# A recurrence phase with another order of its steps, and its triangular solve in blocks of 16 rows that PE joins in pairs

## The chip, the cores and the metric

The kernel runs on one core of a Trainium2 chip. The metric is the device time of one execution in microseconds, as the median of several. Engines are named as in the profile: PE (matmul), DVE (VectorE), ACT (ScalarE), POOL (GpSimd) and SP (SyncE, which here issues most DMAs).

## The reference: what is computed

One decoder layer for 2048 tokens of width 1024. A projection feeds two groups of heads: a state-space mixer (SSD) and an RWKV-7 mixer with 8 heads of 64. Their outputs are projected, normalised and added to the input, and a gated convolutional feed-forward layer with another residual follows. The change lies in the RWKV-7 recurrence, which per head and token is:

```
sa = S @ a_t
S  = S * w_t + outer(sa, b_t) + outer(v_t, k_t)
y  = S @ r_t
```

The kernel computes it by chunks of 64 tokens. Within a chunk the vectors `sa` depend on one another through a strictly lower triangular 64x64 matrix for each head, so a unit triangular system has to be solved for each head and chunk. That is the triangular solve below.

## The kernel before

**Phases.** `phase_R` runs first (RWKV-7 for all tokens), then `phase_S` (the SSD mixer, the output projection) and `phase_F` (feed-forward). They overlap at their seams: generators hand out pieces of S or F that fill PE while R drains.

**Blocks.** R works on 16 blocks of 128 tokens, two chunks of 64 in each, and all 8 heads. The projections ("dense") are made for pairs of blocks: 14 groups of 128 columns of weights `wr`, held in SBUF as two f16 halves, in 28 pieces of 12 matmuls for a pair. `piece()` (a "D" in the plans) issues the next one. `LEAD` (L106) pieces are issued before block 0.

**The order of the work.** PE's instructions keep the order in which the program issues them; it is written out in three strings: `PLAN` (L108) for blocks 0 to 14, `LAST` (L112) for block 15 and `DRAIN` (L116) after it. In a step, `f` is the block whose front half is being made, `b` the block before it, `n` the block four ahead, and a number is a chunk or a part. The other engines' queues are ordered by a scheduler that follows the data; each of them, and SP's DMA queue, then runs in order as well.

**The steps of a block**, as methods of `Block`:

- `load` (L351): normalises the rows of a block four ahead, transposes them on PE in two halves (`norm_T`, L170) and stores them for S; `norm_T` takes a piece in between.
- `low_rank` (L384): 16 matmuls, tanh on ACT, a running sum `cum` on DVE, exponentials `Pi` and `Pv`.
- `keys` (L404), `norm` (L409), `receptance` (L433): normalised keys and the scaled operands `AR` and `BK`; `norm` has one matmul product (`nq`) and much DVE, ACT and POOL work.
- `gram` (L440), for each chunk: 16 matmuls, masked by DVE into `G` (L449).
- `solve` (L453): described next.
- `merge` (L511), steps 0 and 1; `own` (L543), `update` (L562), `state` (L572) for each chunk: the right-hand side `qs`, the solution `UV`, the new state `S0` and the output `ysb`.
- `transposed` (L488), `values` (L498), `gate` (L600), `finish` (L607): transposed keys, values, the output gate, and the group norm of the block with its store to `YR`; `finish` runs ACT, DVE and POOL first and then four transposes on PE (`yt`).

**The solve before.** The 64x64 triangles are cut into blocks of 32 rows. Their 32x32 diagonal blocks (2 chunks x 2 blocks x 8 heads = 32 systems) go from `G` to DRAM (`ATd`, L461, four DMAs) and come back (`atl`, L465, four DMAs) so that each partition holds a whole block; four partitions hold the same block and solve for a quarter of the columns of the inverse each. The start value of `xl` is loaded from DRAM (L470). DVE then runs 31 steps of forward substitution, two operations each: a product into `tmp` (L473) and a sum into `xl` (L476). The result goes through DRAM (`XTd`, L479) to `XT` (L485), four DMAs each. `merge` on PE then makes the off-diagonal 32x32 block of each inverse: DVE transposes the diagonal blocks (`XW`, L517), 32 small matmuls (`pw`, L524), a copy by ACT, 32 more (`po`, L528), a copy.

**Memory.** The names in `R_DENSE` (L76) and its neighbours are tags of SBUF pools in the order in which they lie. When the last dense piece has been issued, the pools of `R_DENSE` are closed, and S and F take their place. `wr` is one tile of 14 groups.

## Time and profile before

| | |
|---|---|
| three runs | 2847.64 us median (2844.04 to 2849.26) |
| the profiled execution | 2854.63 us, span 2852.8 us |
| PE busy | 2516.3 us (88%) |
| DVE busy | 1912.8 us (67%) |
| ACT, POOL busy | 1165.3 us (41%), 1203.1 us (42%) |
| mean granted PE clock | 0.939 |
| the chain that ended last | PE 50%, DVE 22%, POOL 10%, DMA 7% |
| of it, lines of the solve | L476 4%, L473 3% |
| the solve's operations | L473: 496, 134.4 us; L476: 496, 139.1 us |

How to read it: the profile records one execution. Busy time is summed for each engine, and its share of the span is an average over phases that are limited by different things, so the phase has to be looked at by itself. R fills the first third of the span (its first solve starts at 85 us and its last ends at 902 us). A timeline row gives start, duration, engine, line, operation and tiles, and in brackets how long the engine had been idle and which engine's result ended that.

### The profile page before, as it was taken

How to read it: one execution, taken by the hardware profiler on the slowest of the kernel's cores; microseconds unless marked ns; L12 is line 12 of the kernel's file. 1: busy time of each engine (PE TensorE's matmuls, PEld its weight loads, DVE VectorE, ACT ScalarE, POOL GpSimd, SP SyncE). 2: the span in 40 equal slices, each digit the busy share in tenths (PEclk: the TensorE clock that was granted, in tenths of full speed). 3: DMA queues.
4: the chain of work that ended last, by engine and by line, in shares of the span. 5: the costliest groups of instructions: out<-in, count | busy, mean ns of one | idle time of the engine just before them, and what ended most of it. 6: DMA issues, size and time to landing. Idle time of an engine off the chain costs nothing.

```text
span 2852.8 us, 44962 instructions
## 1 busy us (share of the span) xinstructions
PE 2516.3 (88%) x17292; PEld 1517.1 (53%) x17292; DVE 1912.8 (67%) x3512; ACT 1165.3 (41%) x2186; POOL 1203.1 (42%) x1223
## 2 busy tenths in 40 slices
PE   7778878888868899999878898989888899999998
PEld 5567767767655666666544343434333344444443
DVE  6576776776765755666576867787879853554557
ACT  6455554554453433333344454344344343132132
POOL 3233343343332322333265847556574642132234
PEclk8889999989978999999989999999999999999999
DMA  5112112121041211222145443343434643333243
GB/s 198 32 49 51 37 49 52 35 56 47 20 140 49 97 46 57 69 69 89 56 156 170 149 153 126 140 144 141 155 129 142 209 133 104 103 100 103 87 135 126
DMA packets 210951, 285.77 MB, mean 100 GB/s; under 512 B 99632, under 2 KB 118448, under 8 KB 207408
## 3 DMA queue, kind: packets, MB, share of 16 engines
q1 hardware_dynamic: 209152, 280.28, 30.4%
q8 instruction: 135, 2.21, 0.3%
q10 hardware_dynamic: 1584, 2.63, 0.3%
q14 instruction: 80, 0.66, 0.1%
HBM read 180.24 MB, written 102.60 MB: 99 GB/s over the span
## 4 chain that ended last, share of the span: by engine, by line
PE 50%; DVE 22%; POOL 10%; DMA 7%; issue 5%; ACT 4%; SPq 1%; POOLq 0%; DVEq 0%; ACTq 0%
PE u L1272 15%; PE d L1419 9%; PE c L197 5%; PE o L1012 5%; PE d L197 4%; DVE xl L476 4%; DVE tmp L473 3%; PE z L884 2%; POOL fa L1177 2%; DVE a L1309 2%; POOL us L1173 1%; PE gr L445 1%; POOL p L1337 1%; DMA HN<-hT 1%; PE l L1500 1%
## 5 line engine op out<-in xcount | busy, mean ns | idle before, releaser
L1272 PE MATMUL u<-b,w 128*128 128x512 f16 x3696 | 819.4, 384 | 51.0 <-DVE C L1281 37.3
L1272 PEld LDWEIGHTS <-w 128*128 128x128 f16 x3696 | 364.9, 99 | 501.9 <-issue 78.5
L1419 PE MATMUL d<-dw,fa 128*128 128x512 f16 x1512 | 340.3, 384 | 18.5 <-DVE dw L151 18.0
L197 PE MATMUL d<-xt,wr 128*128 128x256 f16 (+1 forms) x2736 | 331.3, 279 | 1.0 <-DVE xt L189 1.0
L197 PEld LDWEIGHTS <-wr 128*128 128x128 f16 x2736 | 268.5, 101 | 62.4 <-issue 25.1
L1419 PEld LDWEIGHTS <-fa 128*128 128x128 f16 x1596 | 158.0, 99 | 225.2 <-issue 37.4
L1281 DVE TENSOR_TENSOR C<-u,C 128x512 f32<-128x512 f32 x220 | 150.7, 685 | 187.0 <-PE u L1272 149.8
L197 PE MATMUL c<-xs,wc 128*128 128x256 f16 x1536 | 193.2, 279 | 0.0
L473 DVE TENSOR_TENSOR tmp<-atl,xl 128x60 f32<-128x60 f32 (+24 forms) x496 | 134.4, 271 | 64.6 <-DMA atl<-ATd 51.6
L1428 DVE TENSOR_TENSOR acc<-d,acc 128x512 f32<-128x512 f32 x212 | 139.9, 682 | 56.1 <-PE d L1419 55.1
L151 DVE SCALAR_TENSOR_TENSOR w<-us,w 128x512 f16<-128x512 f32 x132 | 124.2, 946 | 75.1 <-ACT w L150 74.2
L1309 DVE SCALAR_TENSOR_TENSOR p<-C,fpar,p 128x1024 f32<-128x1024 f32 x88 | 121.9, 1385 | 70.7 <-ACT p L1307 70.5
L197 PEld LDWEIGHTS <-wc 128*128 128x128 f16 x1536 | 151.6, 101 | 29.1 <-issue 4.7
L1177 POOL TENSOR_TENSOR fa<-p,fa 128x512 f16<-128x512 f32 x120 | 151.8, 1276 | 3.9 <-ACT fa L1176 3.9
L1176 ACT ACTIVATE fa<-p 128x512 f16<-128x512 f32 x132 | 79.3, 623 | 176.3 <-DVE p L1313 93.8
L476 DVE TENSOR_TENSOR xl<-xl,tmp 128x60 f32<-128x60 f32 (+24 forms) x496 | 139.1, 280 | 13.8
L150 ACT ACTIVATE w<-us 128x512 f16<-128x512 f32 x132 | 80.3, 622 | 134.7 <-POOL us L1173 98.9
L1309 DVE SCALAR_TENSOR_TENSOR a<-C,fpar,a 128x1024 f32<-128x1024 f32 x88 | 128.2, 1457 | 4.5 <-ACT a L1307 1.7
L582 POOL TENSOR_TENSOR tS<-S,Pi 64x256 f32<-64x256 f32 x64 | 43.3, 677 | 197.6 <-DVE S L592 195.2
L801 DVE SCALAR_TENSOR_TENSOR ca<-rc,cw,ca 128x256 f32<-128x256 f32 x192 | 104.5, 586 | 15.0 <-POOL ca L796 15.0
L1311 POOL COPY fcarry<-C 128x2 f32<-128x2 f32 x88 | 33.4, 379 | 175.2 <-DVE C L1281 174.8
L1306 POOL COPY C<-fcarry 128x2 f32<-128x2 f32 x88 | 39.7, 453 | 155.0 <-ACT a L1307 77.7
(316 smaller groups left out, 4587.8 us busy)
## 6 DMA issues: line engine op xcount, KB each, us to landing
UW<-w SPq DMA_DIRECT2D x154, 256.0 KB, 2.1
w<-UW SPq DMA_DIRECT2D x154, 256.0 KB, 2.7
us<-in_w_u_dram SPq DMA_DIRECT2D x44, 512.0 KB, 3.8
DW<-dw SPq DMA_DIRECT2D x70, 256.0 KB, 2.1
dw<-DW SPq DMA_DIRECT2D x56, 256.0 KB, 3.0
hs<-HN SPq DMA_DIRECT2D x48, 256.0 KB, 3.1
r<-in_w_d_dram SPq DMA_DIRECT2D x10, 1024.0 KB
xin<-in_x_dram SPq DMA_DIRECT2D x17, 512.0 KB, 4.1
```

What stands on the lines that cost most here:

```text
L151: eng.scalar_tensor_tensor(out=lo, in0=src, scalar=scale, in1=hi, op0=ALU.mult, op1=ALU.subtract)
L197: nc.tensor.matmul(ps, w[:, a, kt, :], xt[:, kt, b, cols], start=kt == n == 0, stop=kt == KT - 1 and n == 2)
L473: V.tensor_tensor(out=tmp[:, :m, :n], in0=atl[:, j, j + 1:32].unsqueeze(1).to_broadcast([P, m, n]), in1=xl[:, :m, j:j + 1].to_broadcast([P ...
L476: V.tensor_tensor(out=xl[:, :m, j + 1:32], in0=xl[:, :m, j + 1:32], in1=tmp[:, :m, :n], op=ALU.add)
L801: V.scalar_tensor_tensor(out=acc[:, q], in0=raw[:, q, k:k + TB], scalar=cw[:, g + q, k:k + 1], in1=acc[:, q], op0=ALU.mult, op1=ALU.add)
L1012: nc.tensor.matmul(self.po, l, WO[:, v, (kt + 4) % KT, ds_], start=k == 0, stop=k == 23)
L1177: eng.tensor_tensor(out=lo, in0=src, in1=hi, op=ALU.subtract)
L1272: nc.tensor.matmul(bk[at], self.w[i][:, u, k, :], self.half.b[i][:, k, v, :], start=start and n == 0, stop=n == 11, skip_group_check=True)
L1281: V.tensor_tensor(out=o, in0=ps, in1=a, op=ALU.add)
L1309: V.scalar_tensor_tensor(out=a, in0=c[:, 2 - d:1026 - d], scalar=cw[:, g, 2 - d:3 - d], in1=a, op0=ALU.mult, op1=ALU.add)
L1419: nc.tensor.matmul(ps, pairs[m].a[i][:, u, t * P:t * P + P], ws[n][m][:, v, :], start=new and m == 0 and u == v == 0, stop=m == N - 1 and ...
L1428: V.tensor_tensor(out=acc[j][:, t], in0=ps, in1=acc[j][:, t], op=ALU.add)
```

## The change

- **The solve** works on diagonal blocks of 16 rows. 64 systems of 16 lie on 128 partitions, two partitions to a system, and each solves for half of the columns in 15 steps of two operations. The start value is a constant tile `x0`, copied by POOL. The blocks go to DRAM in eight DMAs, come back in two, the result is stored in two, and eight DMAs bring it to a new tile `DT` (two of them, in turn), in which each group of 32 rows holds two 16x16 blocks on its diagonal.
- **join**, two new steps between solve and merge: DVE transposes all of `DT` by 32x32 blocks into `XD`; 32 matmuls of 32x32 multiply by `G`; DVE masks the product with `lower` so that only the lower left 16x16 quarter stays (`XM`); 32 more matmuls by `DT`, and four DVE sums write the 32x32 diagonal blocks of `XT`. Merge is as before.
- **Order.** `keys` and `low_rank` come first; `finish` runs one block later (prefix `a`: two blocks back); `norm`, `values` and `own.0` come after `join.0`; `gate` stands before the first gram; `load` is split into `prepare` (norm) and two `load` halves, each a step of its own. `X` in `LAST` names the point at which the dense pools close. `LEAD` is 20.
- **Memory.** `wr` becomes 14 tiles, and the order of pools in `R_DENSE` changes. `cum` shares `Pv`; `keys` can so come before `low_rank`.

```diff
-LEAD = 18
+LEAD = 20
 PLAN = """
-f.low_rank b.values D D f.keys D D f.norm D b.own.0 D D f.receptance D b.merge.0 D f.gram.0 b.merge.1 f.gram.1 f.solve
-b.update.0 D b.state.0 D b.own.1 D f.transposed.0 b.update.1 D f.transposed.1 b.state.1 b.gate n.load b.finish
+f.keys f.low_rank D D a.finish D b.join.0 f.norm D b.values D b.join.1 D b.own.0 f.receptance D b.merge.0 b.gate f.gram.0 D
+f.gram.1 b.merge.1 f.solve D n.prepare D b.update.0 D n.load.0 b.state.0 D f.transposed.0 b.own.1 D n.load.1 f.transposed.1
+b.update.1 D b.state.1
 """
 LAST = """
-f.low_rank b.values f.keys b.own.0 f.norm f.receptance D D f.gram.0 f.gram.1 f.solve D D D b.merge.0 D b.merge.1 D
-b.update.0 D b.state.0 D b.own.1 f.transposed.0 D b.update.1 D f.transposed.1 b.state.1 D b.gate D b.finish D
+f.keys f.low_rank a.finish X b.values f.norm b.join.0 b.own.0 f.receptance f.gram.0 f.gram.1 f.solve D D b.join.1 D D b.merge.0 D D b.merge.1
+D b.update.0 f.transposed.0 D b.state.0 f.transposed.1 D D b.own.1 D D b.update.1 b.gate D b.state.1 D
 """
 DRAIN = """
-b.values b.own.0 D D D D D D D D D D b.merge.0 D b.merge.1 D b.update.0 D b.state.0 D b.own.1 D b.update.1 D b.state.1
-b.gate D b.finish D
+b.values a.finish D D D D b.join.0 b.own.0 D D b.join.1 D b.merge.0 D b.merge.1 D b.update.0 D D b.state.0 D b.own.1 D D b.update.1 b.gate
+D D b.state.1 D D D b.finish
 """
...
-                ATd = dr.tile([2, 2, 8, 32, 32], F32, name="ATd" + sf, tag="ATd")
-                XTd = dr.tile([2, 2, 8, 8, 4, 32], F32, name="XTd" + sf, tag="XTd")
+                ATd = dr.tile([2, 4, 8, 16, 16], F32, name="ATd" + sf, tag="ATd")
+                XTd = dr.tile([2, 4, 8, 8, 2, 16], F32, name="XTd" + sf, tag="XTd")
+                for c in range(2):
+                    for b in range(4):
+                        r0 = ub0[c] + 16 * b
+                        nc.sync.dma_start(
+                            ATd[c, b].rearrange("h i j -> i h j"), self.Gv[r0:r0 + 16, c, :, r0:r0 + 16])
+                atl = tl("atl", (16, 16))
+                for q in range(2):
+                    nc.sync.dma_start(
+                        atl[64 * q:64 * q + 64].rearrange("p i j -> p (i j)"),
+                        ATd.rearrange("c b h i j -> (c b h) (i j)"))
+                xl = tl("xl", (8, 16))
+                tmp = tl("tmp", (8, 16))
+                G_.tensor_copy(xl.rearrange("p c i -> p (c i)"), x0)
+                for j in range(15):
+                    n, m = 15 - j, j // 2 + 1
...
+                for q in range(2):
+                    nc.sync.dma_start(
+                        XTd.rearrange("c b h x q i -> (c b h) x q i")[:, :, q, :], xl[64 * q:64 * q + 64])
+                self.XT, DT = XTs[it % 2], DTs[it % 2]
+                for c in range(2):
+                    for b in range(4):
+                        r0, c0 = ub0[c] + 16 * b, 16 * (b % 2)
+                        K.marks["solved"] = nc.sync.dma_start(
+                            DT[r0:r0 + 16, :, c0:c0 + 16], XTd[c, b].rearrange("h x q i -> (x q) h i"))
+
+            def join(self, step):
+
+                DT = DTs[self.it % 2]
+                if step == 0:
+                    self.XD = self.tl("XD", (8, 32), tag="qs")
+                    V.transpose(self.XD.rearrange("p n t -> p (n t)"), DT.rearrange("p n t -> p (n t)"))
+                ps = bank(("pi", "pj")[step] + self.sf, "B").rearrange("p a b -> p (a b)").rearrange("p (n t) -> p n t", t=32)
+                for n in range(8):
+                    for c in range(2):
+                        for b in range(2):
+                            r = slice(ub0[c] + 32 * b, ub0[c] + 32 * b + 32)
+                            l, x = (self.Gv[r, c, n, r], self.XD) if step == 0 else (self.XM[r, n, :], DT)
+                            nc.tensor.matmul(
+                                ps[r, n, :], l, x[r, n, :], start=True, stop=True, tile_position=(r.start, r.start))
+                if step == 0:
+                    self.XM = self.tl("XM", (8, 32), tag="XW")
+                    V.tensor_tensor(
+                        out=self.XM, in0=ps[:, 0:8], in1=lower.unsqueeze(1).to_broadcast([P, 8, 32]), op=ALU.mult)
+                    return
                 for c in range(2):
                     for b in range(2):
...
+                        r = slice(ub0[c] + 32 * b, ub0[c] + 32 * b + 32)
+                        V.tensor_tensor(
+                            out=self.XT[r, :, 32 * b:32 * b + 32], in0=ps[r, 0:8], in1=DT[r], op=ALU.add)
...
+                if step == "X":
+                    filling[0] = True
+                    for c in reversed(front):
+                        c.close()
+                    next(F)
+                    next(filler)
+                    continue
                 who, name, *a = step.split(".")
                 a = [int(v) for v in a]
...
+                i = it + {"f": 0, "b": -1, "a": -2, "n": 4}[who]
+                blk = blocks[i] if 0 <= i < iters else None
```

More of the change, by code (lines that the diff above doesn't have):

```diff
@@ L72, in tile @@
         return self.pools[tag].tile(shape, dt, name=name, tag=tag, bufs=bufs)
-R_DENSE = ("xin", "xt", "raw", "wr", "A0", "tv0")
+R_DENSE = (
+    *(f"wr{g}" for g in range(7, 14)), "xt", "raw", "xin", *(f"wr{g}" for g in range(7)), "A0", "tv0",
+)
 R_RIGHT = (
-    "mus omu w0h a0h ka5 kam tiny carry vr gnv gnr ss pnv pnr", "XT0 XT1 qs S0_0 S0_1 tS ysb yln tg",
-    "g2 cmat GL XW", "A1", "tv1", "UV", "G", "BT", "Pi", "AR",
+    "mus omu w0h a0h ka5 kam tiny lnj carry vr gnv gnr ss pnv pnr", "XT0 XT1 qs S0_0 S0_1 tS ysb yln tg",
+    "g2 cmat GL XW lower DT0 DT1", "A1", "tv1", "UV", "G", "BT", "Pi", "AR",
 )
-R_FRONT = ("wl WX", "atl xl tmp", "BK", "sq kkn thw tha Pv")
+R_FRONT = ("wl WX", "atl xl tmp x0", "BK", "sq kkn thw tha Pv")
 S_LEFT = (
@@ L167, in rsqrt_cols, with norm_rows @@
     return r
-def norm_T(tc, K, work, psp, pstag, src, g, dst, col, sfx, between=None, junk=None):
+def norm_rows(tc, K, work, src, sfx, junk):
     nc = tc.nc
@@ L252, in phase_R @@
         XTs = [wk.tile([P, 8, 64], F32, name=f"XT{i}") for i in range(2)]
-        for t in S0 + XTs:
+        DTs = [wk.tile([P, 8, 32], F32, name=f"DT{i}") for i in range(2)]
+        x0 = wk.tile([P, 128], F32, name="x0")
+        lower = wk.tile([P, 32], F32, name="lower")
+        for t in (x0, lower):
+            G_.memset(t, 0.0)
+        for q in range(2):
+            G_.memset(x0[64 * q:64 * q + 64, q:128:18], 1.0)
+        rows = wk.tile([P, 4], F32, name="XD0", tag="qs")
+        V.tensor_reduce(
+            out=rows, in_=K.ident.rearrange("p (a b) -> p a b", b=32)[:, :, 16:32], op=ALU.add, axis=AX.X)
+        row = wk.tile([P, 1], F32, name="XM0", tag="XW")
+        V.tensor_reduce(out=row, in_=rows, op=ALU.add, axis=AX.X)
+        V.tensor_copy(lower[:, 0:16], row[:, 0:1].to_broadcast([P, 16]))
+        for t in S0 + XTs + DTs:
             G_.memset(t, 0.0)
@@ L258, in phase_R @@
         ub0 = (64, 0)
-        W = wk.tile([P, NG, 2, KT, P], F16, name="wr")
+        W = [wk.tile([P, 2, KT, P], F16, name=f"wr{g}") for g in range(NG)]
         def load_w(g):
@@ L303, in units @@
                         for k in (0, 4):
[L304 removed]
+                            dense(tc, ps[:, q], W[g + q], self.xt, slice(0, 256), range(k, k + 4))
                             if q and k:
@@ new lines, in solve @@
+                atl = tl("atl", (16, 16))
+                for q in range(2):
+                    nc.sync.dma_start(
[7 more added lines that the diff above has]
+                    V.tensor_tensor(
+                        out=tmp[:, :m, :n], in0=atl[:, j, j + 1:16].unsqueeze(1).to_broadcast([P, m, n]),
+                        in1=xl[:, :m, j:j + 1].to_broadcast([P, m, n]), op=ALU.mult)
+                    V.tensor_tensor(
+                        out=xl[:, :m, j + 1:16], in0=xl[:, :m, j + 1:16], in1=tmp[:, :m, :n], op=ALU.add)
@@ new lines, in solve @@
+                for q in range(2):
+                    nc.sync.dma_start(
[6 more added lines that the diff above has]
+                            DT[r0:r0 + 16, :, c0:c0 + 16], XTd[c, b].rearrange("h x q i -> (x q) h i"))
@@ L468, in solve @@
-                xl = tl("xl", (8, 32))
-                tmp = tl("tmp", (8, 32))
-                nc.sync.dma_start(xl.rearrange("p c i -> p (c i)"), K.cst_dram[:, COFF["x0"][0]:COFF["x0"][1]])
-                for j in range(31):
-                    n, m = 31 - j, j // 4 + 1
-                    V.tensor_tensor(
-                        out=tmp[:, :m, :n], in0=atl[:, j, j + 1:32].unsqueeze(1).to_broadcast([P, m, n]),
-                        in1=xl[:, :m, j:j + 1].to_broadcast([P, m, n]), op=ALU.mult)
-                    V.tensor_tensor(
-                        out=xl[:, :m, j + 1:32], in0=xl[:, :m, j + 1:32], in1=tmp[:, :m, :n], op=ALU.add)
@@ L645, in phase_R @@
                 for it in range(2):
-                    blocks[it].load()
+                    blocks[it].arrive()
         pieces = (None for p in pairs for _ in p.units())
@@ L661, in phase_R @@
             if n in (9, 14):
-                blocks[2 if n == 9 else 3].load()
+                blocks[2 if n == 9 else 3].arrive()
         for it in range(iters + 1):
```

95 lines of the change are left out of this document (35 added, 60 removed).

## The prediction

> **What bounds the kernel now.** I read the page first: in its busy tenths the first third of the span, the recurrence phase, is the place where PE, DVE and ACT are all well occupied and none is full. Then I read the timeline for the period of that phase, the same timeline for one turn of its loop, the waits of PE, the windows of the solve, and the chain of waits for what one step costs PE. All columns of a timeline are: start, us, engine, line, operation, output<-input, count, and the idle time before it with its releaser.
>
> The first three rows are the masking of the second gram matrix of blocks 0, 14 and 15.
>
> ```profile
> 76.89 1.29 DVE L449 TENSOR_TENSOR G<-gr,cst 128x512 f32<-128x512 f32 x2 [1.04 <-PE gr L445]
> ...
> 807.64 1.29 DVE L449 TENSOR_TENSOR G<-gr,cst 128x512 f32<-128x512 f32 x2 [1.04 <-PE gr L445]
> ...
> 872.97 1.29 DVE L449 TENSOR_TENSOR G<-gr,cst 128x512 f32<-128x512 f32 x2 [1.75 <-PE gr L445]
> ```
>
> From block 0 to 14 it takes (807.64 - 76.89) / 14 = 52.2 us a block, and 65.3 us from 14 to 15. Now one turn, from the second gram of one block to that of the next:
>
> ```profile
> 547.20 1.75 PE L445 MATMUL gr<-AR,BK 64*128 64x128 f32 x16 [0.15 <-DVE G L449]
> ...
> 556.63 0.19 DVE L473 TENSOR_TENSOR tmp<-atl,xl 128x31 f32<-128x31 f32 x1 [3.68 <-DMA atl<-ATd]
> ...
> 587.21 0.16 DVE L476 TENSOR_TENSOR xl<-xl,tmp 128x8 f32<-128x8 f32 x1
> ...
> 587.40 2.55 SPq L479 DMA_DIRECT2D XTd<-xl  x4
> ...
> 591.34 1.95 SPq L485 DMA_DIRECT2D XT<-XTd  x4
> ...
> 594.26 0.43 DVE L517 STREAM_TRANSPOSE XW<-XT 32x256 f32<-32x256 f32 x1 [0.54 <-DMA XT<-XTd]
> ...
> 594.75 0.69 PE L524 MATMUL pw<-XW,G 32*32 32x32 f32 x30 [0.93 <-DVE XW L517]
> ...
> 598.72 1.75 PE L445 MATMUL gr<-AR,BK 64*128 64x128 f32 x16 [0.15 <-DVE G L449]
> ```
>
> Gram ends at 548.95; the solve's first operation runs at 556.63, 7.7 us later (store to DRAM, load back). The solve lasts to 587.37. Its result is stored and brought back by 594.26 (6.9 us), transposed, and b.merge.0 (pw) can run at 594.75, where PE had waited. Behind pw in PE's order stand the two grams, and the second ends at 600.47: 51.5 us for the turn, 30.7 of them the solve. Why is the solve so long?
>
> ```profile
> 556.63:587.37 30.74, 18.10 (x62) 0.89 0.19 61
> 817.78:861.75 43.97, 18.50 (x62) 0.54 0.58 189
> ```
>
> ```profile
> 556.63:587.37 30.74, 25.30 (x237) 20.45 (x236) 28.88 (x86) 19.11 (x38) 13.99 (x15) 0.89 0.19 61
> 817.78:861.75 43.97, 22.84 (x150) 17.69 (x148) 38.03 (x86) 25.58 (x42) 16.92 (x15) 0.54 0.58 189
> ```
>
> The first pair of rows is the solve's own operations in the solve of block 9 and of block 14, the second pair the whole engine. Of 30.74 us DVE works 28.88, 18.10 in the 62 operations of the solve (0.29 each) and 10.8 in others. So DVE is the bound of that stretch. But not in every block is the solve what PE waits for:
>
> ```profile
> PE yt L619 <- POOL ysb L615: 31.9, 13, 5.4
> PE nq L414 <- ACT sq L407: 24.9, 13, 4.0
> PE vt L502 <- ACT thw L393: 19.6, 13, 2.3
> PE pt L183 <- DVE xin L185: 17.9, 11, 5.5
> PE pw L524 <- DVE XW L517: 13.2, 10, 3.2
> ```
>
> In 13 blocks PE waited only 13.2 us for the solve (pw), yet 94.3 us for finish (yt), norm (nq), low_rank (vt) and the loading of a new block (pt). Most of these inputs come through the same DVE queue or through ACT and POOL behind it. In the blocks with no wait at pw the lost time stands there instead. Both kinds end at 52 us.
>
> **The change, part by part.** The terms of PE, from the chain (start, us net of overlap, what) of the same turn:
>
> ```profile
> 543.29 0.62 PE pw L524 x32
> 543.91 1.42 PE d L197 x12
> 545.33 1.14 PE gr L445 x16
> ...
> 548.95 1.07 PE pu L567 x16
> ...
> 551.44 0.61 PE pS L587 x16
> 552.06 1.07 PE pq L595 x16
> ...
> 554.54 1.08 PE pq L552 x32
> 555.62 1.09 PE pq L556 x8
> ...
> 558.02 0.44 PE bt L495 x4
> ...
> 566.12 0.67 PE pt L183 x4
> ```
>
> A D (12 dense matmuls) is 1.42, a 32-tile pass such as merge 0.62, gram 1.14, update 1.07, state 0.61 + 1.07, own 1.08 + 1.09, a transposition of a key block 0.44, half of a load 0.67. Three more come from elsewhere:
>
> ```profile
> 569.05 0.66 PE L619 MATMUL yt<-cst,ysb 128*128 128x128 f32 x4 [2.28 <-POOL ysb L615]
> ```
>
> ```profile
> 373.95 1.12 PE L414 MATMUL nq<-sq,cst 128*128 128x512 f32 x2 [3.67 <-ACT sq L407]
> 374.91 2.42 PE L197 MATMUL d<-xt,wr 128*128 128x256 f16 x12
> ```
>
> ```profile
> 859.41 2.07 PE L414 MATMUL nq<-sq,cst 128*128 128x512 f32 x2 [4.87 <-ACT sq L407]
> ...
> 907.76 1.05 PE L502 MATMUL vt<-cmat,tv 128*128 128x128 f32 x8
> 908.65 1.02 PE L507 MATMUL bo<-A,cst 128*128 128x512 f32 x2
> 909.60 1.15 PE L552 MATMUL pq<-UV,G 64*64 64x64 f32 x32
> ```
>
> finish's transposes take 0.66; norm's product 374.91 - 373.95 = 0.96; b.values 909.60 - 907.76 = 1.84. The gate I take like own's second half, 1.09 (eight matmuls of the same shape), low_rank as 8/12 of a D, 0.95.
>
> *The solve.* 30 operations take the place of 62, on 128 partitions as before. Shares of time are not cut by shape: what counts is the number. In the same company 30/62 x 30.74 = 14.9 us; as the widest shapes fall away, I take 14.0. Bounds: 30 x 0.29 = 8.7 with DVE all to itself, and 30/62 x 43.97 = 21.3 in the crowd of block 14.
>
> *Its transfers.* Each stays a DRAM round trip, in pieces of 16 floats and no longer of 32. Store of the grams: eight DMAs for four, load back: two for four; half of the stores are issued before the second gram, so I keep 7.7. Store of the solution: two issues of 2.55/4 = 0.64 fewer, unless an issue of twice the pieces takes twice as long: 3.94 (587.40 to 591.34) becomes 2.7 to 3.9, taken 3.3. Back to SBUF: eight issues at 1.95/4 = 0.49 for four, 2.92 becomes 4.9. SP works in order: the row loads, XN and YR stores stand in the same queue, and a store that waits there holds up the eight. The load of xl's start leaves SP and becomes one POOL copy, hidden in the 7.7.
>
> *Ready for join.0* (L): after the second gram, 7.7 + 14.0 + 3.3 + 4.9 + 0.5 for one DVE transposition (0.43 for 32 partitions of the old) = 30.4 us, for 45.8 up to pw.
>
> *What follows it to the next gram* (M). Here the change lengthens the loop. join.0 0.62, norm 0.96, five D 7.1, values 1.84, join.1 0.62, own 2.17, merge.0 0.62, gate 1.09, two grams 2.28: 17.3 us in PE's order, where it was 5.7. The DVE work of the joins (one product, four sums, two transpositions, some 3 us by the 0.43 rows) lies beside 5.6 us of PE between join.0 and join.1 and 5.0 between join.1 and merge.0. If DVE is over 2 us behind, it shows as a wait.
>
> *What PE has to do meanwhile*: merge.1, six D, update, state, two load halves, two transpositions, own, update, state, then low_rank, two D, finish, one D: 0.62 + 9 x 1.42 + 2.14 + 3.36 + 1.34 + 0.88 + 2.17 + 0.95 + 0.66 = 24.9 us. finish waits for POOL as before: in the row of 569.05 PE sat 2.28 us with a gate, a D and two load halves ahead (3.85 us); now low_rank and two D stand there (3.79), so 2.3 us of wait. PE comes to join.0 27.2 us after the gram, and the solve 3.2 later: PE waits there, and behind it in its queue every D of the block. The waits of norm and values go, since keys and low_rank now stand far ahead; the wait of loading shrinks, prepare being apart.
>
> *The clock.* After the wait of 3.67 before nq the next D took 2.42 in place of 1.42; after 0.93 before pw it did not. I add 1.0. The Trainium skill (TensorE: Matmul & The Clock Gate, Part 1) says that the clock halves after about 3.4 us of idle PE and comes back after as much sustained work; by it, as an estimate, a long wait would cost 1.7 and the period be 0.7 longer (rival B takes this further, from rows). The granted clock of 0.54 in block 14's crowded solve agrees with it.
>
> Period: 30.4 + 17.3 + 1.0 = 48.7, so 3.5 us less than 52.2; fourteen times 3.5 = **49**.
>
> *Block 14 to 15* (65.3 us). With S's weights being split on DVE at the same time, DVE does 38.03 of 43.97 us, 18.50 in the solve. Without half of that, 9.5 us shorter; X, which opens S's buffers, stands later, and join.0 and own.0 now stand between the solve and the gram (2.8 us), while nq's wait of 4.87 goes from behind it. I take **10**, between 0 and 20.
>
> *Start.* LEAD 20: two D more before block 0, one fewer inside: **+2** (0 to 3). More memsets and three small DVE operations lie beside the weight loads. wr in fourteen tiles sets weight buffers free earlier; in block 14 to 15 only, in the bound above. The drain after block 15 has 14 + 4 D of S's products ahead of join.0, over 23 us, and PE stays busy there.
>
> Sum: -49 - 10 + 2 = -57. The profiled execution took 2854.63 us (span 2852.8 and 1.8 around it), 7.0 above the median of the runs, 2847.64. So 2797.6 by the profile's time, **2791 us** as a median. All that comes after (S, F) is bound by PE and moves earlier as a whole.
>
> **The rivals.**
>
> A: the solve hides. If its 30 operations find DVE half free, 10 us, L is 26.4 and below the 27.2 of PE; then the period is PE's own 24.9 + 2.3 + 17.3 = 44.5, rounded to 45: 14 x 7.2 = 101, 14 at block 15 (the 4 us more), +2: 2734.6. For it: others take 10.8 of 30.74, and several of them (low_rank's scan, norm's work) now come after the solve. Against: loads, states and finish's sum remain in it.
>
> B: the clock falls at the wait of join.0 and stays down. Cold, nq took 2.07 (row of 859.41) for 0.96, D 2.42 for 1.42. If join.0, nq, D and values (4.84 us) all take 1.7 times as long, the loss is 3.4, the period 51.1: 14 x 1.1 = 15, 6 at block 15 (10 less the loss), +2: 2828.6. For it: 2.3 and 3.2 us of wait stand only one D apart. Against: after most waits of under 2 us a D is unchanged.
>
> C, slower: small pieces. The present landing times:
>
> ```profile
> ATd<-G SPq DMA_DIRECT2D x64, 32.0 KB, 1.7
> XTd<-xl SPq DMA_DIRECT2D x64, 32.0 KB, 2.0
> XT<-XTd SPq DMA_DIRECT2D x64, 32.0 KB, 2.0
> ```
>
> These three hops move 128-byte pieces; the new ones move 64-byte pieces. If they land in twice the time, 1.7 + 2.0 + 2.0 = 5.7 us, L is 36.1, PE waits 9 us at join.0 with all its dense work behind it, and with the cold loss of B the period is 36.1 + 17.3 + 3.4 = 56.8: 14 x 4.6 = +64, 0 at block 15, +2: 2914. It turns to a loss once L passes 52.2 - 17.3 - 1.0 = 33.9, 3.5 above my sum. Against it: the bytes in all halve for the stores and the number of pieces stays. The Trainium skill (DMA: Bandwidth & Descriptors, Specifications) says that pieces below 512 bytes do not run at line rate and cost a read-modify-write; both sizes are below, so by it alone the landing would stay, and no run here shows 64 bytes.
>
> D: no change. The waits of yt and pt are POOL's and DVE's order and not the solve's; if they grow to fill what is gained, the period stays 52: 2848.
>
> **How the numbers follow.** Forecast 0.56, A 0.18, B 0.14, C 0.07, D 0.05. The range leaves out C and D and the lower part of A: 2732 to 2830. Something like 0.2% (5.7 us) is about what a measurement of this kernel can tell from no change. Faster: forecast, A and B, 0.88; D is the same, 0.05; slower 0.07.
>
> **What would show it.** In the profile after: 480 operations each on the lines of tmp and xl become 240; some 14 us from first to last; masking of the second gram every 48 to 49 us; PE waits at join.0 for the transposition of DT by 2 to 4 us, hardly at nq and vt; yt still by 2. No wait at join.0 means A; D at 2.4 after join.0 means B; DT's transfers landing after 4 us mean C. I am wrong if the period is unchanged, or if the gain lies behind the recurrence phase.

## The result, and the profile after

| | before | after |
|---|---|---|
| median of 8 runs each | 2848.45 us (2844.04 to 2853.31) | 2868.67 us (2859.37 to 2875.42) |
| the profiled execution, its span | 2854.63, 2852.8 us | 2869.60, 2867.8 us |
| PE, DVE, POOL busy | 2516.3, 1912.8, 1203.1 us | 2532.0, 1819.8, 1224.3 us |

The change makes the kernel slower: the ratio is 1.0061, interval 1.0045 to 1.0077. The forecast was 2791 us.

First the timeline, the rows that answer to the three of before: masking of the second gram matrix of blocks 0, 14 and 15.

```profile
77.84 1.27 DVE L476 TENSOR_TENSOR G<-gr,cst 128x512 f32<-128x512 f32 x2
...
837.15 1.28 DVE L476 TENSOR_TENSOR G<-gr,cst 128x512 f32<-128x512 f32 x2
...
883.16 1.29 DVE L476 TENSOR_TENSOR G<-gr,cst 128x512 f32<-128x512 f32 x2 [1.75 <-PE gr L472]
```

From block 0 to 14 it now takes 759.31 us, 54.24 a block, where it was 730.75 and 52.20. From 14 to 15 it takes 46.0 us, where it was 65.3. So the steady blocks lose 28.6 us, the last one wins 19.3, and the start costs 0.95 (77.84 for 76.89). That is 10.2 of the 15.0 us by which the span grew; the other 4.8 appear after block 15's mask and were not followed further. The loss sits in the period of the steady blocks.

Is DVE relieved, as meant? The windows over these 14 periods, of before and then of after (length, then busy time and instructions of PE, PEld, DVE, ACT and POOL, the granted clock, DMA):

```profile
76.89:807.64 730.75, 600.34 (x6782) 497.32 (x6780) 509.81 (x1435) 365.87 (x741) 265.98 (x293) 0.91 0.17 43
```

```profile
77.84:837.15 759.31, 613.72 (x8561) 509.11 (x8558) 429.30 (x1086) 373.14 (x750) 287.14 (x308) 0.89 0.14 35
```

Yes: DVE does 429.30 us of work where it did 509.81, 5.75 less for each block, and yet the stretch is longer. What was taken away did not lie on the path that sets the period any more. What does? Here is the timeline of one turn of after, from the second gram of one block to that of the next (the same block as the turn shown of before):

```profile
564.59 1.19 PE L472 MATMUL gr<-AR,BK 64*128 64x128 f32 x16
...
573.78 0.18 DVE L500 TENSOR_TENSOR tmp<-atl,xl 128x15 f32<-128x15 f32 x1 [1.01 <-DMA atl<-ATd]
...
583.38 0.17 DVE L503 TENSOR_TENSOR xl<-xl,tmp 128x8 f32<-128x8 f32 x1
...
583.80 2.66 SPq L506 DMA_DIRECT2D XTd<-xl  x2
591.33 3.64 SPq L512 DMA_DIRECT2D DT<-XTd  x8
...
594.40 1.11 PE L671 MATMUL yt<-cst,ysb 128*128 128x128 f32 x4 [6.37 <-POOL ysb L667]
595.30 2.76 PE L202 MATMUL d<-xt,wr 128*128 128x256 f16 x12
...
596.37 0.45 DVE L520 STREAM_TRANSPOSE XD<-DT 128x256 f32<-128x256 f32 x1
...
598.00 1.08 PE L527 MATMUL pi<-XD,G 32*32 32x32 f32 x64
...
618.43 1.16 PE L472 MATMUL gr<-AR,BK 64*128 64x128 f32 x16
```

The second gram ends at 565.78. The solve starts 8.0 us later and is over at 583.55, after 9.8 us. Its store to DRAM is issued at 583.80, but the loads back only at 591.33, 7.5 us later. The transposed `XD` is ready at 596.82, 31.0 us after the gram. PE comes to join.0 (`pi`) still later, at 598.00, because it had waited 6.37 us for the finish step (`yt`), and the D behind that wait took 2.76 us instead of 1.47. From join.0 to the end of the second gram 21.6 us pass. L = 32.2 and M = 21.6 give 53.8 for this block.

The waits of PE between 135 and 840 us (sum, times, longest):

```profile
PE yt L671 <- POOL ysb L667: 85.9, 13, 7.8
PE zg L655 <- ACT XW L586: 21.2, 13, 2.8
```

`yt` is 6.6 us a block on the mean of 13 blocks, where it was 31.9 us in 13 waits (2.5 a block); `zg` is a wait that the profile of before does not have. PE does not wait for `XD` at join.0 in any of these blocks. Now why finish is late. The chain of waits of after through the same stretch (start, us, what):

```profile
584.45 0.59 ACT ysb L650
585.07 1.15 ACT thw L420 x4
586.37 1.52 POOL thw L422
587.92 1.24 DVE Pv L423
589.22 1.69 POOL gnr L169
590.91 0.40 POOL tm L446
591.35 1.32 POOL tm L446 x3
592.90 1.46 POOL ysb L667
```

And the same step in the profile of before, ACT's rows and then POOL's:

```profile
563.11 0.59 ACT L598 ACTIVATE ysb<-pq 64x512 f32<-64x512 f32 x1 [1.09 <-PE pq L595]
...
565.50 0.20 POOL L165 TENSOR_SCALAR gnv<-vr 128x8 f32<-128x8 f32 x1 [1.10 <-DVE vr L613]
565.79 1.66 POOL L166 TENSOR_TENSOR gnr<-gnv,mhalf 128x8 f32<-128x8 f32 x1
567.53 1.47 POOL L615 TENSOR_TENSOR ysb<-ysb,gnr 128x512 f32<-128x512 f32 x1
```

Before, finish took from 563.11 to 569.00 with only its own operations in the chain: 5.9 us. After, it takes from 584.45 to 594.36: 9.9 us. Between its first copy and its end stand low_rank's tanh on ACT (L420), the addition to it on POOL (L422), the running sum on DVE (L423) and the `tm` products of norm on POOL (L446), none of which finish needs. Those queues run in order, so finish waits behind them. PLAN alone does not put them there: it has norm behind finish, and the run h1 below keeps low_rank ahead of finish in PLAN and still has finish's first operations ahead of low_rank's on ACT and POOL. What the rows show is that in this kernel low_rank's matmuls follow PE's last product of the state at once (first `zw` at 584.34, first tanh at 585.07, finish's square `y` only at 586.08). The 4.0 us more are the 4.1 by which `yt`'s wait grew (6.37 for 2.28).

### The profile page after: what moved, and what is told of

Its sections match the earlier page's. It is cut to its first block, busy times and chain, and to the rows that moved or that the text cites. A ratio compares the mean times of both kernels' runs of the same rounds, so it can differ in the third digit from the quotient of the medians.

```text
span 2867.8 us, 48821 instructions
## 1 busy us (share of the span) xinstructions
PE 2532.0 (88%) x19340; PEld 1533.6 (53%) x19340; DVE 1819.8 (63%) x3099; ACT 1167.6 (41%) x2188; POOL 1224.3 (43%) x1245
## 4 chain that ended last, share of the span: by engine, by line
PE 49%; DVE 16%; POOL 13%; ACT 8%; DMA 6%; issue 5%; SPq 1%; POOLq 0%; DVEq 0%; ACTq 0%
PE u L1321 15%; PE d L1468 10%; PE c L202 5%; PE o L1061 5%; PE d L202 3%; PE z L933 2%; POOL fa L1226 2%; POOL us L1222 1%; PE gr L472 1%; POOL p L1386 1%; DMA HN<-hT 1%; DVE a L1358 1%; PE l L1549 1%; DVE tv L342 1%; DMA atl<-ATd 1%
## 5 line engine op out<-in xcount | busy, mean ns | idle before, releaser
L202 PE MATMUL d<-xt,wr 128*128 128x256 f16 (+1 forms) x2736 | 351.1, 286 | 1.1 <-DVE xt L194 1.1
L202 PEld LDWEIGHTS <-wc 128*128 128x128 f16 x1536 | 152.8, 102 | 30.4 <-issue 4.8
L154 DVE SCALAR_TENSOR_TENSOR w<-us,w 128x512 f16<-128x512 f32 x132 | 118.4, 904 | 70.2 <-ACT w L153 65.2
L845 POOL TENSOR_SCALAR ca<-rc,cw,cb 128x256 f32<-128x256 f32 x64 | 50.6, 799 | 117.2 <-ACT rc L841 117.2
L476 DVE TENSOR_TENSOR G<-gr,cst 128x512 f32<-128x512 f32 x64 | 41.1, 684 | 90.8 <-PE gr L472 90.8
```

Of the source, the lines that this page charges most:

```text
L154: eng.scalar_tensor_tensor(out=lo, in0=src, scalar=scale, in1=hi, op0=ALU.mult, op1=ALU.subtract)
L202: nc.tensor.matmul(ps, w[:, a, kt, :], xt[:, kt, b, cols], start=kt == n == 0, stop=kt == KT - 1 and n == 2)
```

## The experiments

Every kernel is an edit of the kernel after. The period is read as above, from the end of the second mask of block 0 to that of block 14, divided by 14. The ratio is to runs of the kernel before on the same chip; these had medians of 2845.48 to 2851.22, so differences between the times of two rows are good to some 3 to 6 us. e2 and f1 leave out 28 of the 30 operations of each solve, so theirs are not times of the whole layer.

| run | median, us | ratio to before, interval | period, us |
|---|---|---|---|
| after | 2868.67 | 1.0061 (1.0045 to 1.0077) | 54.24 |
| e1_finish_later | 2867.91 | 1.0055 (1.0040 to 1.0070) | 54.56 |
| e2_short_solve | 2851.28 | 1.0002 (0.9984 to 1.0020) | 53.93 |
| e3_old_order | 2815.20 | 0.9871 (0.9851 to 0.9890) | 50.38 |
| e4_old_solve | 2911.27 | 1.0205 (1.0188 to 1.0222) | 56.96 |
| f1_both | 2797.22 | 0.9814 (0.9795 to 0.9834) | 48.78 |
| f3_gate | 2827.23 | 0.9918 (0.9893 to 0.9944) | 51.86 |
| f4_fill | 2878.07 | 1.0095 (1.0075 to 1.0115) | 54.73 |
| f5_mixed | 2818.62 | 0.9886 (0.9857 to 0.9914) | 50.80 |
| g1_gate_only | 2806.18 | 0.9865 (0.9844 to 0.9887) | 50.40 |
| g2_old_order_tuned | 2809.86 | 0.9878 (0.9857 to 0.9898) | 50.43 |
| g3_store_later | 2801.87 | 0.9846 (0.9825 to 0.9867) | 50.12 |
| h1_gate_and_store | 2798.75 | 0.9827 (0.9806 to 0.9848) | 49.13 |
| h2_store_only | 2849.12 | 0.9995 (0.9985 to 1.0006) | 53.05 |
| h3_finish_first | 2910.38 | 1.0216 (1.0199 to 1.0233) | 56.64 |

### Which half of the change loses: the solve or the order?

**e3_old_order**: the new solve and the joins, in the order of before.

```diff
-LEAD = 20
+LEAD = 18
-f.keys f.low_rank D D a.finish D b.join.0 f.norm D b.values D b.join.1 D b.own.0 f.receptance D b.merge.0 b.gate f.gram.0 D
-f.gram.1 b.merge.1 f.solve D n.prepare D b.update.0 D n.load.0 b.state.0 D f.transposed.0 b.own.1 D n.load.1 f.transposed.1
-b.update.1 D b.state.1
+f.low_rank b.values D D f.keys D D f.norm b.join.0 D b.own.0 b.join.1 D D f.receptance D b.merge.0 D f.gram.0 b.merge.1 f.gram.1 f.solve
+b.update.0 D b.state.0 D b.own.1 D f.transposed.0 b.update.1 D f.transposed.1 b.state.1 b.gate n.prepare n.load.0 D n.load.1 b.finish
...
```

> The new solve and joins in the old order of the steps (finish last in its own block, low_rank and values first, keys behind; the joins stand between norm and own, where six or more D lie between solve and join). Theory 1: the order is what cost time and the shorter solve is worth something by itself: faster than before, 2800 to 2835 us. Theory 2: joins and smaller transfers cost as much as the 32 operations saved: 2845 us or more.

**e4_old_solve**: the new order, with the solve of before and no joins.

```diff
-f.keys f.low_rank D D a.finish D b.join.0 f.norm D b.values D b.join.1 D b.own.0 f.receptance D b.merge.0 b.gate f.gram.0 D
+f.keys f.low_rank D D a.finish D f.norm D b.values D D b.own.0 f.receptance D b.merge.0 b.gate f.gram.0 D
...
```

> The old solve by 32 rows with the new order, the joins left out of the plans. Theory 1: a solve 20 us longer no longer fits between gram and merge in an order that puts finish behind low_rank: PE waits both at yt and at merge, period 57 us or more, 2895 us or more. Theory 2 in its other form (the joins are what costs): without joins the period falls below 54, the time below 2868.

Measured: 2815.20 and 2911.27 us. The new solve wins 36 us in the old order (2851.22 beside it) and 43 in the new one (2911.27 to 2868.67). The new order loses 53 with the new solve (2868.67 against 2815.20) and 60 with the old. The two halves of the change have opposite signs, and the order is the larger. (e3 also puts the joins where the old order has room for them.) PE's waits in e4:

```profile
PE yt L646 <- POOL ysb L642: 69.4, 11, 6.9
PE pw L551 <- DVE XW L544: 30.7, 17, 4.4
```

The wait of `yt` is there with the old solve too, so it belongs to the order. The last line, PE's wait for the result of the solve at merge, goes with a longer solve.

### Two chains of the same length

**e1_finish_later**: finish behind values, so that its wait cannot stand ahead of join.0.

```diff
-f.keys f.low_rank D D a.finish D b.join.0 f.norm D b.values D b.join.1 D b.own.0 f.receptance D b.merge.0 b.gate f.gram.0 D
+f.keys f.low_rank D D D b.join.0 f.norm D b.values a.finish D b.join.1 D b.own.0 f.receptance D b.merge.0 b.gate f.gram.0 D
```

> Only finish is moved in PLAN, from ahead of the first join to behind values. Theory 1 (PE stands in its own queue behind finish's transposes, 6.6 us a block, and that wait sets when the first join is issued): the wait at yt falls under 1 us, PE comes to the first join about 5 us earlier and waits there 1 to 3 us for DT; the period falls from 54.2 to 50 to 51 us and the time to 2810 to 2825 us. Theory 2 (the DRAM round trip of the solve sets the period whatever stands before it): the wait moves from yt to the first join, the period stays at 53 to 54, the time within 6 us of 2868.

**e2_short_solve**: one step of the solve for 15; the other 14 are left out.

```diff
-                for j in range(15):
+                for j in range(1):
```

> The forward substitution is cut from 15 steps to one, so 28 of 30 DVE operations a block are left out; all transfers and joins stay. Theory 1: DT only comes earlier for a PE that is not waiting for it, so the period falls by under 1.5 us (less work on DVE beside finish) and the time stays above 2845 us. Theory 2: the round trip is 8 us shorter, the period falls by 5 us or more, the time to about 2795.

**f1_both**: the two edits together.

> Finish moved behind values and the forward substitution cut to one step, the two edits that changed little alone (2867.9 and 2851.3 us), together. Leaves out 28 of the 30 solve operations of a block. Theory 3 (two chains of equal length, POOL's for finish and the solve's round trip, both let PE go on about 30 us after the gram; each hides what is taken from the other): PE reaches the first join at 24 us, the period falls to 47 to 49 us, the time to 2770 to 2795. Theory 4 (what PE has to do in its own order is the bound and the waits only fill it): period 53 us or more, 2845 us or more.

Measured: 2867.91 (nothing gained, as its second theory had it), 2851.28 (17 us) and 2797.22 (71 us, just above the 2770 to 2795 expected). The waits of PE in the three, between 135 and 760 us: e1, e2, f1.

```profile
PE pi L527 <- DVE XD L520: 71.9, 12, 8.3
```

```profile
PE yt L671 <- POOL ysb L667: 91.5, 12, 8.8
```

```profile
PE pj L527 <- ACT yln L674: 26.8, 11, 2.8
...
PE yt L671 <- POOL ysb L667: 5.5, 6, 2.6
```

In e1 the wait at `yt` is gone and PE waits 6.0 us a block at join.0 for DT instead. In e2 DT is early and PE waits 7.6 a block at `yt`. Only with both away does the period fall, by 5.5 us to 48.78. So behind the second gram stand two chains of about the same length, solve to DT and state.1 to finish; each covers what is taken from the other. One experiment at a time would have called both harmless.

Two things go with that. The first turn, from block 0 to 1, in which PE waits for the solve alone, is 39.7 us in e2 and 40.2 in f1 for 52.7; it holds 13 of e2's 17 us. From block 1 to 14 the period is 54.35 in after, 55.02 in e2 and 49.45 in f1. And the cover is not the whole account of e1. On the mean of blocks 1 to 13 PE comes to join.0 29.8 us after the end of the second gram where after has 32.7, but from there to the end of the next second gram it takes 24.8 us for 21.4, with finish and a wait of `pj` for its bank now in that stretch. In f1 the two parts are 23.1 and 26.2.

### The gate, and the filling around it

**f3_gate**: the gate goes to the end of the turn, the D between the grams ahead of them, and merge.1 between them.

```diff
-f.keys f.low_rank D D a.finish D b.join.0 f.norm D b.values D b.join.1 D b.own.0 f.receptance D b.merge.0 b.gate f.gram.0 D
-f.gram.1 b.merge.1 f.solve D n.prepare D b.update.0 D n.load.0 b.state.0 D f.transposed.0 b.own.1 D n.load.1 f.transposed.1
-b.update.1 D b.state.1
+f.keys f.low_rank D D a.finish D b.join.0 f.norm D b.values D b.join.1 D b.own.0 f.receptance D b.merge.0 D f.gram.0
+b.merge.1 f.gram.1 f.solve D n.prepare D b.update.0 D n.load.0 b.state.0 D f.transposed.0 b.own.1 D n.load.1 f.transposed.1
+b.update.1 D b.state.1 b.gate
```

> The gate goes from ahead of the first gram to behind the state of chunk 1, and the D between the two grams goes ahead of them; nothing else. Theory 3 with its second half (the stretch from the first join to the second gram's mask, 23.8 us where 17.3 and 1.3 for the mask were forecast, stands on the loop whole): the wait for the copy of pw (1.6 us), the gate (1.1 to 1.4) and the late mask (up to 2.4 in every second block) leave the loop, period down by 3 to 4 us, 2812 to 2830. Theory 4: PE has the same work, period within 1 us, 2855 or more.

**g1_gate_only**: only the gate.

```diff
-f.keys f.low_rank D D a.finish D b.join.0 f.norm D b.values D b.join.1 D b.own.0 f.receptance D b.merge.0 b.gate f.gram.0 D
+f.keys f.low_rank D D a.finish D b.join.0 f.norm D b.values D b.join.1 D b.own.0 f.receptance D b.merge.0 f.gram.0 D
...
-b.update.1 D b.state.1
+b.update.1 D b.state.1 b.gate
```

> Half of the run that gained 41 us: the gate goes behind the state of chunk 1, the D between the two grams stays. Gate theory (its product waits for the copy of pw and stands with 1.1 to 1.4 us on the loop, and it shortens the wait at yt by the work it puts ahead): at least two thirds of the gain, period 52.5 or less, 2840 us or less. Mask theory (the D between the grams brings its shift ahead of the second mask into DVE's queue, up to 2.4 us in every second block): under one third, 2855 us or more.

Measured: 2827.23 and 2806.18. The gate alone gives 56 us by the ratios (62 by the times), 3.8 a block; what f3 moved besides, the D and merge.1, had cost 15 to 21 of that. So the second thought behind f3, that the D between the grams holds up the second mask and should go, is refuted. The timeline of after shows what the gate did where it stood:

```profile
613.28 1.44 PE L655 MATMUL zg<-GL,g 128*128 128x128 f32 x8 [0.85 <-ACT XW L586]
614.65 2.08 PE L472 MATMUL gr<-AR,BK 64*128 64x128 f32 x16
616.66 1.84 PE L202 MATMUL d<-xt,wr 128*128 128x256 f16 x12
```

The products of join, merge, gate and finish go to banks of PSUM, the memory that matmuls write to; these have one tag, `B`, of which there is one buffer. The gate's product could not start before ACT had copied merge.0's out of it: 0.85 us here, 1.6 on the mean of 13 blocks (21.2 us in all). Gate, gram and D then took 1.44, 2.08 and 1.84 us, where the chain of before had 1.09, 1.14 and 1.42; the granted clock was 0.76 from 613.3 to 614.7, 0.50 to 616.7 and 0.80 to 618.5. With g1's order the wait for `yt` falls too:

```profile
PE yt L671 <- POOL ysb L667: 32.7, 13, 6.9
```

That is 2.5 a block for 6.6, where the gate put in front of it is only 1.09 us of PE work. The rest of the fall is that finish's chain (first copy on ACT to `ysb` on POOL) got shorter, 7.0 us on the mean for 10.1. With the gate between state.1 and low_rank on PE, finish's operations come first on ACT and POOL, though PLAN still has low_rank ahead of finish; the rows of h1, which has the same order there, are below.

**f4_fill**: two D from behind join ahead of finish.

```diff
-f.keys f.low_rank D D a.finish D b.join.0 f.norm D b.values D b.join.1 D b.own.0 f.receptance D b.merge.0 b.gate f.gram.0 D
+f.keys f.low_rank D D D D a.finish D b.join.0 f.norm D b.values b.join.1 D b.own.0 f.receptance b.merge.0 b.gate f.gram.0 D
```

> Two of the five D behind the first join go ahead of finish, so that 11 D and not 9 lie between solve and join. Theory 3: they fill waits that are there anyhow, and the stretch behind the join is 2.8 us shorter: period 51 to 52 us, 2825 to 2840 us. Theory 4: the same work in another place, within 6 us of 2868.

Measured: 2878.07, 9 us more than after and outside both expectations. The wait at `yt` fell to 43.6 us in all (135 to 780 us), but the way from join.0 to the end of the second mask stayed at some 23.5 us, with 26.5 us of wait at `pw` in 21 places. M is not PE's work alone: norm's products and the four sums of the join go through DVE's queue one behind the other (in the chain of after from `kkn` at 603.49 to `XW` at 611.26), and PE's D are only what lies beside it. The half of the theory that took M for PE work fell.

**f5_mixed**: e3's plan and LEAD with after's LAST (finish taken out) and DRAIN.

> PLAN and LEAD of the run with the new solve in the old order, LAST and DRAIN of the changed kernel. If gains add: the period of 49.4 us of that run and the last block of the changed kernel (46.0 us for 14 to 15 where that run had 51.0, and 54.4 for 13 to 14 where it had 58.1): 5 to 9 us below 2815, so 2806 to 2810. If the last block's gain came from the order ahead of it: 2815 or more.

**g2_old_order_tuned**: e3's order with keys behind low_rank, one D put ahead of values and another ahead of finish, where it waited (the plan; LAST and DRAIN as in f5).

```diff
+f.low_rank f.keys D b.values D D f.norm b.join.0 D b.own.0 b.join.1 D D f.receptance D b.merge.0 D f.gram.0 b.merge.1 f.gram.1 f.solve
+b.update.0 D b.state.0 D b.own.1 D f.transposed.0 b.update.1 D f.transposed.1 b.state.1 b.gate n.prepare n.load.0 D n.load.1 D b.finish
```

> The new solve in the old order, with the work that fills its two remaining waits moved: keys behind low_rank, a D between low_rank and values, two D and not one in the second half of the load ahead of finish; LAST and DRAIN of the changed kernel. If PE's waits at yt (3.0 us a block) and vt (1.4) are what is left above PE's own work: period 50.4 to 47.5 or 48.5, 2775 to 2795 us. If they come back elsewhere, as two of the moves before did: 2805 to 2820.

Measured: 2818.62 and 2809.86. f5 and e3 differ by 3.4 us in time and 0.0015 in the ratio, so LAST and DRAIN change little; PLAN does it. (The 49.4 us that f5's expectation gives as e3's period is 50.38 when read as in the table.) In g2 the wait at `yt` fell to 25.4 us and 33.3 came up at `pw` (135 to 780 us): the D that fill one wait uncover the next, as in f4.

### The store of the rows ahead of the solve's

**g3_store_later**: f3, and the second load half (with its 1 MB store XN and 512 KB load) at the end of the turn (the diff is against f3).

```diff
-b.merge.1 f.gram.1 f.solve D n.prepare D b.update.0 D n.load.0 b.state.0 D f.transposed.0 b.own.1 D n.load.1 f.transposed.1
-b.update.1 D b.state.1 b.gate
+b.merge.1 f.gram.1 f.solve D n.prepare D b.update.0 D n.load.0 b.state.0 D f.transposed.0 b.own.1 D f.transposed.1
+b.update.1 D b.state.1 n.load.1 b.gate
```

> On the order with gate and D moved (2827 us): the second half of the load, and so the 1 MB store of XN and the 512 KB load behind it, goes to the end of the turn. If the solve's store of 32 KB lands late in every second block because these transfers are under way (6.7 us from its issue to the issue of DT's, where it is 2.8 in the other blocks): 2.8 in all blocks, the wait at the first join there falls by up to 3 us, 2805 to 2818 us. If the two are unrelated: 6 to 7 us stay in every second block, 2823 to 2832.

**h2_store_only**: the same move, in after and by itself.

> Only the second half of the load moved in the changed kernel, the gate left. Closing theory: finish's transposes hold PE until 30 us after the gram in this order, so DT's earlier landing gains nothing: within 8 us of 2868. If the collision alone cost time: 2845 or less.

**h1_gate_and_store**: g1's move of the gate and the load half at the end of the turn.

> The gate behind the state (2806 us) and the second half of the load at the end of the turn, with the D between the grams left where it is. Closing theory (the forecast period of 48.7 us was missed by the gate, 3.9 us, and by the store of XN that the shorter solve runs into, 1.7): period 48.3 to 49, 2780 to 2792 us. If the two take the same wait away: 2800 to 2808.

Measured: 2801.87 for g3 (a little below the 2805 to 2818 expected), 2849.12 for h2 and 2798.75 for h1. The period falls by 1.7 (f3 to g3), 1.2 (after to h2) and 1.3 (g1 to h1). h2 brings 20 us, against the expectation that it would bring almost nothing as long as finish's chain is the longer. Its wait at `yt` is 6.05 a block and hardly shorter. So the store's place costs 1.2 to 1.7 us a block. In h2 the gain is not an earlier join.0: PE comes to it 32.6 us after the gram for 32.7 (mean of blocks 1 to 13), though DT's transposition ends 2.7 us earlier (26.9 for 29.6). It lies in the stretch behind join.0, 20.4 us for 21.4; through which effect stays open. How the store delays DT is plain in SP's queue, after and then before:

```profile
582.93 0.35 SPq L220 DMA_DIRECT2D xin<-in_x_dram  x1
583.32 0.43 SPq L390 DMA_DIRECT2D XN<-xt  x1
```

```profile
570.16 0.43 SPq L368 DMA_DIRECT2D XN<-xt  x1
```

In after both are issued right ahead of XTd (583.80) in every second block from 1 to 9, and from XTd's issue to DT's it takes 6.7 to 8.1 us in those blocks, 2.8 to 4.4 in the others. In before XN went out 17 us ahead of XTd (587.40). With h1's plan it is 2.8 to 3.9 in every block.

h1 is the fastest of the kernels that do the whole solve. It was expected at 2780 to 2792 us and took 2798.75 (four runs, 2794.76 to 2807.74), 1.7% less than before. Its timeline, one turn:

```profile
517.41 1.18 PE L472 MATMUL gr<-AR,BK 64*128 64x128 f32 x16
...
537.15 0.63 ACT L664 ACTIVATE y<-ysb 128x512 f32<-128x512 f32 x1
...
538.50 0.62 ACT L420 ACTIVATE thw<-zw,w0h 128x128 f32<-128x128 f32 x2
...
541.28 1.51 POOL L422 TENSOR_SCALAR thw<-thw 128x512 f32<-128x512 f32 x1
...
542.75 1.04 POOL L667 TENSOR_TENSOR ysb<-ysb,gnr 128x512 f32<-128x512 f32 x1
...
543.85 0.66 PE L671 MATMUL yt<-cst,ysb 128*128 128x128 f32 x4 [2.37 <-POOL ysb L667]
544.34 1.47 PE L202 MATMUL d<-xt,wr 128*128 128x256 f16 x12
549.16 1.05 PE L527 MATMUL pi<-XD,G 32*32 32x32 f32 x64 [3.35 <-ACT yln L674]
...
566.47 1.18 PE L472 MATMUL gr<-AR,BK 64*128 64x128 f32 x16
```

From the end of the gram (518.59) to join.0 30.6 us, from there to the end of the second gram (567.65) 18.5: 49.1, where 48.7 was forecast for the change. Finish's square `y` now stands ahead of low_rank's tanh on ACT, and of low_rank's operations only the addition L422 stands ahead of `ysb` on POOL: the chain takes 7.3 us (536.53 to 543.79) for 9.9. What is left to gain shows in it: 2.37 us at `yt`, and 3.35 at `pi`, where the join's product waits until ACT has copied `yt` out of the PSUM bank that both use. That copy runs only from 547.62 to 549.11, 3.1 us after `yt` ended, since low_rank's two exponentials (L427 and L428, from 546.42) stand ahead of it in ACT's queue.

**h3_finish_first**: finish ahead of low_rank, so that ACT's and POOL's queues have its operations first.

```diff
-f.keys f.low_rank D D a.finish D b.join.0 f.norm D b.values D b.join.1 D b.own.0 f.receptance D b.merge.0 b.gate f.gram.0 D
+f.keys D D a.finish f.low_rank D b.join.0 f.norm D b.values D b.join.1 D b.own.0 f.receptance D b.merge.0 b.gate f.gram.0 D
```

> Only low_rank and finish change places. If finish's chain is long because low_rank's tanh on ACT and its addition on POOL stand ahead of it in those queues: the wait at yt falls from 6.4 to 3 or 4 us though 0.95 us less of PE work stands ahead of it; the time stays within 10 us, since DT holds the first join in every second block. If the chain is long for another reason (gate, state): 6.5 us or more of wait.

Measured: 2910.38, 42 us more than after, where a time within 10 us was expected. PE's waits:

```profile
PE yt L671 <- POOL ysb L667: 40.4, 11, 4.8
PE pw L576 <- DVE XW L569: 32.5, 16, 5.4
```

The wait at `yt` fell to 3.7 a block, as it should if low_rank's operations ahead of it are its cause. But low_rank itself now comes late, norm and the grams behind it, and the way from join.0 to the mask grew from about 24 to 27 to 30 us. In the turn of block 9 low_rank's running sum ends 23.4 us after the gram in after, 26.7 in g1 and 32.6 in h3, so putting finish first makes low_rank later, by a little in g1 and by much here. The order of before has gate, a D and two load halves ahead of finish and low_rank behind it, and its chain took 5.9 us.

## Why the prediction was wrong

**The step that failed** is the one that carried a wait over from before: "finish waits for POOL as before ... so 2.3 us of wait." It compared PE's work ahead of finish, 3.79 for 3.85 us, and that part holds: PE came to `yt` after 22.25 us of work (588.03 - 565.78), where the forecast has 24.9 less `yt` and the D behind it, 22.8. What it left out is what the moved steps put into the other queues: operations of low_rank and norm now stand ahead of finish's on ACT, POOL and DVE, and finish's chain takes 9.9 us for 5.9. Two edits that take them out of the way confirm it: in g1 the chain is 7.0 us and the wait 2.5 a block, in h3 6.5 and 3.7. The wait measured 6.37, and with it the granted clock fell, from 1.00 (566 to 588 us) to 0.50 (594.40 to 599.0): `yt` took 1.11 for 0.66, D 2.76 for 1.47, another 1.75. PE's arrival at join.0 became 32.2 us for the 27.2 forecast, later than DT, so it and no longer the solve set that part of the turn.

**M, the second step**, and the larger share of the miss: "17.3 us in PE's order", with 1.0 for the clock, measured 21.6. On the mean of blocks 1 to 13 the turn is 32.7 and 21.4 us, 2.3 and 3.1 above the forecast's 30.4 and 18.3. The 3.3 missing in the traced block are the gate's wait for the bank (0.85), its product and the gram and D behind it at the lower clock (0.35 + 0.94 + 0.42), and 0.8 of wait for the join's sums at `pw`. The gate's place carries much of both parts: in g1, where it is gone from M, the means are 30.6 and 19.6. Without the gate's 1.09 the forecast of M would be 17.2; h1 has 18.5 in the traced turn and 18.0 on the mean. So the prediction added M up from PE's own work and put the wait for a shared bank at nothing; a wait for DVE's sums it named but did not price, and its 1.0 for the clock is for one fall, where the clock fell twice in this turn, at `yt` and ahead of the gram.

**L, the sum that came out right by two errors.** The solve took 9.8 us, not 14.0, and 7.7 to 11.1 in all blocks but the first:

```profile
573.78:583.55 9.77, 5.96 (x30) 0.00 (x0) 1.00 0.01 2
```

```profile
573.78:583.55 9.77, 9.54 (x124) 8.36 (x123) 8.84 (x36) 4.42 (x9) 1.69 (x3) 1.00 0.01 2
```

The first row is the solve's own 30 operations: 5.96 us, 0.20 each. The second is the engine: DVE was busy 8.84 of 9.77. Scaling the old stretch by the count was too dear, since the other work was partly somewhere else by then. The store to DT was forecast at 3.3 and took 7.5 in this block, for the collision with XN, which the prediction named in general ("a store that waits there holds up the eight") and did not price. `XD` was ready 31.0 us after the gram for 30.4; in the blocks without the collision it was 25.6 to 30.4. That is hardly earlier, since in every second block the mask, which DVE does behind other work, starts up to 2.5 us after its gram, and the solve with it.

**What was right.** The waits at `nq` and `vt` went. The small pieces (rival C) do not land in twice the time:

```profile
ATd<-G SPq DMA_DIRECT2D x128, 8.0 KB, 1.5
...
DT<-XTd SPq DMA_DIRECT2D x128, 8.0 KB, 1.7
XTd<-xl SPq DMA_DIRECT2D x32, 32.0 KB, 3.6
```

1.5 and 1.7 us for 8 KB in 64-byte pieces, where 32 KB in 128-byte ones landed in 1.7 and 2.0. Only XTd moves the same 32 KB as before: its 3.6, for 2.0, is the median of 2.2 to 6.1, with and without XN ahead, and in h1, where XN is out of the way, it is 2.2. The Trainium skill (DMA: Bandwidth & Descriptors, Specifications) puts the least size for line rate at 512 bytes. Both sizes lie below it; how they compare there, only these rows show. Block 14 to 15 was forecast at -10 and gave -19.3, inside its bounds; the start +2 and gave +0.95.

**The rivals.** The sign that the prediction names for A, no wait at join.0, appeared, but not for A's reason: the solve took the 10 us that A gives it and `XD` still came after 25.6 to 31.2 us, and PE was later than that, with waits that A's 44.5 does not have. B's clock did fall, but by the wait at `yt`: at join.0 it was already 0.50, back at 1.00 from 600.6 on, and it fell again ahead of the gram. D's mechanism, that waits behind POOL and DVE grow to fill what is gained, is the nearest: e1, e2 and f1 show it. It was given 0.05 and a period of 52, because it was thought of as a limit and not as queues that get longer. No rival had the new order costing more than the new solve brings. The stated bound, a loss once L passes 33.9, was worked out with an M of 18.3; the loss came with PE at join.0 after 32.2 us and an M of 21.6, together 53.8 for 52.2.

The forecast time, 2791, is within 8 us of h1, the change without the gate's place and the load's. That is partly luck: there PE comes to join.0 after 31.1 us on the mean and M is 18.0, but it still waits at `yt` and at `pi`, and `XD` is ready after 26.8.

## What to carry to other kernels

When a step is moved in one engine's order, write down what it puts into every other in-order queue and who stands behind it there; a wait of before is no figure for a place with other neighbours. When two chains end at the same point, take both away in one run, since each alone shows nothing. Fill work moved ahead of one wait leaves another uncovered: what counts is the sum over the loop.

## What the runs showed of the hardware

**The clock after a wait.** In the kernel after, all 13 waits at `yt` between 100 and 840 us lasted 5.93 to 7.85, and each time `yt` took 1.11 to 1.12 (0.66 at the full granted clock) and the next D 2.45 to 2.77 (1.47): some 1.7 us a wait. In h1 the five waits of 2.35 to 2.42 cost nothing (0.66, 1.47), while after those of 2.54 to 2.67 the next D took 1.92 to 2.77. The length of the wait does not settle it: in g1 three of six waits of 2.53 to 2.56 cost nothing, and in before `yt` took 1.11 after a wait of only 1.39 (at 206.61 us), where the granted clock was already 0.50 after a wait of 5.48 just ahead. The Trainium skill (TensorE: Matmul & The Clock Gate, Part 1) gives about 3.4 us of idle PE for the fall and as much work for the way back; the price agrees, as an estimate of half of 3.4, but here the loss could begin after a wait of 2.54.

**A small POOL operation that runs as long as a DVE one.** The groups of POOL, `gnv` of finish, before and after (count, busy, mean ns):

```profile
L165 POOL TENSOR_SCALAR gnv<-vr 128x8 f32<-128x8 f32 x12 | 2.4, 202 | 13.3 <-DVE vr L613 12.2 <-DVE tmp L473 1.1
```

```profile
L168 POOL TENSOR_SCALAR gnv<-vr 128x8 f32<-128x8 f32 x12 | 14.1, 1174 | 1.0
```

The same operation on 128x8 takes 202 ns in before and 1174 in after. In the turn shown it ran from 587.97 to 589.14, and DVE's running sum from 587.92 to 589.14. The Trainium skill (SBUF — State Buffer, section SBUF: two separate sides) says that the two engines share a pair of ports and that one of them is blocked until the other's instruction ends; these rows agree, and the new order puts the two side by side in every block. In g1 and h1, where finish's operation comes ahead of the running sum, the mean is 236 and 217 ns. The difference between before and after is 1.0 of the 4.0 us by which finish got longer.
